# A gated-delta scan on one core: QK loaded and multiplied later, the first units' loads reordered, the last products in halves

## The chip, the cores and the metric

One core of a Trainium2 chip runs the whole program. The metric is the device time in microseconds of one execution; lower is better. The engines are TensorE (PE, with its weight loads PEld), VectorE (DVE), ScalarE (ACT), GpSimd (POOL) and SyncE (SP), which here issues all loads and stores. Each engine works through its own instruction stream in order and waits for others by semaphores.

## What is computed

One layer of a hybrid backbone on 128 context and 2048 latent tokens of width 1024 (17 tiles of 128 tokens): modulated norm, one input projection, a bidirectional chunked gated DeltaNet with 4 heads of 128 beside a gated spatial MLP, an output projection, and a squared-ReLU MLP of width 4096. The change concerns the DeltaNet, whose core in the reference is, for each head, direction and chunk (chunks of 64 in the reference; the kernel works on 128 tokens at a time):

```python
a_mat = where(strict, (k_beta @ k.T) * decay, 0)
sol = triangular_solve(a_mat + eye, [v * beta, k_beta * exp(g)])     # u, w
qk = (q @ k.T) * decay
def step(S, xs):
    v_new = u_c - w_c @ S
    o = qd @ S + qk_c @ v_new
    S = S * exp(gl) + kd.T @ v_new
```

and the last rows of the output, `y + ga2 * (relu(h @ w_ff1)**2 @ w_ff2)` followed by a norm.

## The kernel before

PE multiplies float32 as two rounded halves: `mm3` (L242, L243, L244) issues three matmuls, high x high, the low half of one side (L243) and the low half of the other (L244), into one PSUM bank. Names that end in H and L are such halves (`wH`, `wL`, `hH`, `hL`, `opH`, `opL`); ACT makes the high one by a copy, DVE the low one by a subtraction.

By time, the program has four stages. Up to about 440 us: modulation, norm, and the q, k and v projection with its convolution; KK = k k^T and QK = q k^T of each tile are left in DRAM (`kk_d`, `qk_d`), as are the running sums of the log decays (`g_d`). From about 440 to 1230: the scan, which this text is about. From 1230 to 2592: the two products of the MLP.

The scan has 34 units, 17 tiles forward and then 17 backward; a unit takes some 22 us. Unit i has a preparation, which does not depend on the state, and four chain steps, which do.

- Loads for the preparation (`prep_loads`): `gb`, the sums of the tile's log decays broadcast to all partitions, `KK` and `QK`.
- ACT makes the decays `E` = exp(-|gb - g|) (four Abs by head at L1035, one exp of 128x512 at L1036). POOL cuts it into the strict triangle `Es` (L1038) and the inclusive one, in place in `E` (L1040). DVE multiplies `KK` by beta and `Es` (four products, L1048), POOL sets the diagonal (L1050), ACT rounds to `AH` (L1053), DVE forms `X` (L1054), PE transposes it (L1060) and ACT copies it to `Y` (L1062).
- Five levels s = 2 to 32 of the triangular inverse: PE (L1080), DVE's masked `P` (L1084), PE (L1092, L1094), ACT's copies of `Y` and `X` (L1095, L1096). At s = 2, DVE also multiplies `QK` by `E` (L1098). A sixth level, a correction `R` and the result `T` follow (L1110 to L1139).
- Chain: vt and o from the state (L1151, L1143); `vs` and `vn` (L1164, L1166); the new state `S` (L1178); and QK times vn, added to o (L1192 to L1197). All these quads of matmuls have line L1011.

`KK`, `E` and `Es` share one tag "e" with four buffers, and `QK` has three buffers. Preparation PSUM tiles are `pd`, four banks.

Between these, as filler for PE, run the projections for gate, v and u of the gMLP (`f2`, PSUM tiles `pj` and `pm`, with loaded halves `hH`, `hL` of the normed tile, L1237), and from the backward units on the output projection (`wH,oH`), the norm for the MLP and the first operands of the MLP (`opH`, `opL`, L904 and L905).

The order of all this is set by a list: `at(time, fn)` puts a step at a time in units, the list is sorted, and the code is issued in that order. A scheduler that simulates times then sets each engine's order from it, taking what is ready; a tile's buffers count as ready when their last reader is done. `after_weights(f, names, engines)` adds that f's instructions stand behind those of an earlier group on the named engines. The loads of unit i's preparation stand at i - 3, those of unit 0 at -11.85; `f2[0][0]`, the loads of hH and hL of tile 0, at -9.

At the very end, the last MLP product of the last tile sums four groups q = 0 to 3, of four operands each, into one bank of 512 columns; q = 3 is done in two halves of 256 columns, and after each half `part` (in `final_last`) does the final sums on DVE and ACT.

Of the kernel before, what the change touches and what calls it, by code (L numbers as in the profile page):

```python
# [8 lines left out]
F32 = mybir.dt.float32  # L9
# [4 lines left out]
ALU = mybir.AluOpType  # L14
# [3 lines left out]
P = 128  # L18
# [34 lines left out]
PL = 0  # L53
# [12 lines left out]
def hybrid_step(  # L66
# [143 lines left out]
    done = {}  # L210

    def here():
        return len(tc.nc.cur_bb.bb.instructions)
# [24 lines left out]
    def mm3(ps, trip, first=True, last=True, more=False):  # L238

        n = len(trip)  # L240
        for i, (lh, ll, rh, rl) in enumerate(trip):
            T.matmul(ps, lh, rh, start=first and i == 0, stop=False, skip_group_check=more)  # L242
            T.matmul(ps, lh, rl, start=False, stop=False, skip_group_check=more)  # L243
            T.matmul(ps, ll, rh, start=False, stop=last and i == n - 1, skip_group_check=more)  # L244
# [716 lines left out]
    with ExitStack() as ph:  # L961
# [20 lines left out]
        def q32(tag, bufs=1, pool=None):  # L982
            return (pool or dl).tile([P, 4, P], F32, tag=tag, name=tag, bufs=bufs)

        def s32(name):
            return pp.tile([P, 4, P], F32, tag="e", name=name, bufs=NE)
# [14 lines left out]
        def unit(t, d):  # L1001
# [11 lines left out]
            def prep_loads():  # L1013
                u["gb"] = load_rows(g_d, t, d)
                u["KK"] = s32("KK")
                load(out=u["KK"], in_=kk_d[t])
                u["QK"] = q32("QK", 3)
                load(out=u["QK"], in_=qk_d[t])

            def scan_loads():  # L1020
# [9 lines left out]

            @prep.append
            def _():
                e = s32("E")
                for h in range(H):
                    A.activation(e[:, h, :], u["gb"][:, h, :], AF.Abs, scale=-1.0, bias=col(gcol, h))  # L1035
                A.activation(e, e, AF.Exp, scale=-1.0)  # L1036
                es = s32("Es")
                G.affine_select(out=es, in_=e, pattern=[[0, 4], [-sg, P]], compare_op=ALU.is_gt, fill=0.0,  # L1038
                                base=0, channel_multiplier=sg)
                G.affine_select(out=e, in_=e, pattern=[[0, 4], [sg, P]], compare_op=ALU.is_ge, fill=0.0,  # L1040
                                base=0, channel_multiplier=-sg)
                u["Es"], u["E"] = es, e
# [22 lines left out]
            def level(s):  # L1065

                def half(ap, i):
                    return ap.rearrange("p h (a t b) -> p h a t b", t=2, b=s)[:, :, :, i, :]

                def packed(p, i):  # L1070
                    return p[:, :, i * 64 : i * 64 + 64].rearrange("p h (a b) -> p h a b", b=s)

                yi = 1 - d

                @prep.append
                def _():
                    p = pd()
                    pp, y = packed(p, 0), half(u["Y"], yi)
                    for h in range(H):
                        T.matmul(pp[:, h], u["AH"][:, h, :], y[:, h], start=True, stop=True)  # L1080
                    u["P"] = pms[s]
                    if t == 0:
                        V.tensor_copy(pms[s], identq)
                    V.tensor_tensor(out=half(u["P"], yi), in0=pp, in1=half(bc4(sm[s]), yi), op=ALU.mult)  # L1084

                @prep.append
                def _():
                    p = pd()
                    py, px = packed(p, 0), packed(p, 1)
                    y, x, pm = half(u["Y"], yi), half(u["X"], 1 - yi), half(u["P"], yi)  # L1090
                    for h in range(H):
                        T.matmul(py[:, h], u["X"][:, h, :], pm[:, h], start=True, stop=True)  # L1092
                    for h in range(H):
                        T.matmul(px[:, h], u["P"][:, h, :], x[:, h], start=True, stop=True)  # L1094
                    A.copy(y, py)  # L1095
                    A.copy(x, px)  # L1096
                    if s == 2:
                        V.tensor_tensor(out=u["QK"], in0=u["QK"], in1=u["E"], op=ALU.mult)  # L1098

            for s in (2, 4, 8, 16, 32):  # L1100
                level(s)
# [56 lines left out]
            @scan.append  # L1158
            def _():
                p = pd()  # L1160
                quad(p, u["T"], u["vt"])
                u["vs"] = q32("vs", 1)
                cols = eglg[:, t, d * 4 : d * 4 + 4].unsqueeze(2).to_broadcast([P, 4, P])
                V.tensor_tensor(out=u["vs"], in0=p, in1=cols, op=ALU.mult)  # L1164
                u["vn"] = q32("vn", BT)
                A.copy(u["vn"], p)  # L1166

            @scan.append
            def _():
# [30 lines left out]

            u["t"], u["d"] = t, d
            u["prep"], u["scan"] = prep, scan
            u["prep_loads"], u["scan_loads"] = prep_loads, scan_loads
            return u

        units = [unit(t, 0) for t in range(NT)] + [unit(t, 1) for t in [0] + list(range(NT - 1, 0, -1))]
# [181 lines left out]
        def at(time, fn, kind=None):  # L1388
            events.append((time, len(events), fn, kind))
# [13 lines left out]
        def after(i):  # L1403
# [4 lines left out]
            load(out=s0, in_=state_delta[0, 0, d].rearrange("h k v -> k h v"))  # L1408
            units[i + 1]["s0"] = s0

        def after_weights(f, names, engines):

            start = here()
            f()
            for name in names:
                behind(name, start, engines)

        p2, p3 = WINDOWS[:8], WINDOWS[8:]
        for i, u in enumerate(units):
            w = p2 if i <= NT else p3  # L1420
            at(i - 3 if i > PL else -11.85, u["prep_loads"])
            at(i - 1, lambda i=i, u=u: after_weights(u["scan_loads"], LATER.get(i, ()), (mybir.EngineType.SP,)))
            u["prep"][:2] = [lambda i=i, f=f: after_weights(f, AHEAD_OF.get(i, ()), (mybir.EngineType.Activation,
                                                                                    mybir.EngineType.DVE))
                             for f in u["prep"][:2]]
            n = len(u["prep"])
            for j, st in enumerate(u["prep"]):
                at(i - w[0] + (j + 0.5) * (w[0] - w[1]) / n if i or j > 9 else -11.6 if j < 2
                   else 0.2 * j - 8.15, st, "prep")
            spread(i + w[2], i + w[3], [scan_step(i, f) for f in u["scan"]], "chain")  # L1430
            if i in (0, NT):
                at(i + w[2] + (w[3] - w[2]) * 0.7, lambda i=i: after(i))
            if i >= NT:
                at(i, lambda u=u: o_loads(u))
                first, second = o_steps(u)
                spread(i + p3[4], i + p3[5], first, "fill")
                spread(i + p3[6], i + p3[7], second, "fill")
                if u["t"] > 8:
                    st = h2_steps(u["t"], pj, fraw, w512, fpart, fhalf, lambda u=u: u["x2"])
                    spread(i + p3[8], i + p3[9] + 0.2, st[:5], "fill")  # L1440
                    spread(i + p3[9] + 0.2, i + p3[9] + 2.1, st[5:], None)
# [10 lines left out]
            flat += [(KT * n + j, st) for j, st in enumerate(main)]  # L1452
            flat += [(KT * n + KT + j + (0.5 if n >= HT else -0.5), st) for j, st in enumerate(later)]
        flat = [st for _, st in sorted(flat, key=lambda e: e[0])]
        at(-9, f2[0][0])
        engines = (mybir.EngineType.Activation, mybir.EngineType.DVE)
        for j, st in enumerate(flat[:NF]):
            g, k = divmod(j, KT + 1)
# [53 lines left out]
    def bank():  # L1512
        return psq.tile([P, 512], F32, tag="f", name="f", bufs=8)

    def add(out, a, b, op=ALU.add):
        V.tensor_tensor(out=out, in0=a, in1=b, op=op)  # L1516
# [268 lines left out]
    def final_last(t, y):  # L1785
# [12 lines left out]

        def part(ps, h):
            c = slice(256 * h, 256 * h + 256)  # L1800
            add(x[0][:, c], ps[:, c], ga[0][:, c], ALU.mult)
            add(y[0][:, c], x[0][:, c], y[0][:, c])
            A.activation(x[0][:, c], y[0][:, c], AF.Square, accum_out=ss[:, 2 * h : 2 * h + 1])
            if h == 0:
                V.scalar_tensor_tensor(out=ss[:, 3:4], in0=ss[:, 0:1], scalar=1.0 / D, in1=ss[:, 3:4], op0=ALU.mult,
                                       op1=ALU.add)
# [135 lines left out]
                    s_next(AHEAD + e // 2 - 1, True) if e // 2 < 3 else None  # L1942


    pending = []
    rest = ps = None
    for m, (n, i, u, q) in enumerate(todo):
        us = products[n][1]
# [11 lines left out]
            elif i == 2:  # L1960
                rest = final(0, [y0[0], y0[1]]) if u == 8 else final(pairs[u][0], [acc["x", u], acc["u", u]])
        h, lo = sops.pop(m)
        if m == len(todo) - 1:
            for e in range(2):
                c, e2 = slice(256 * e, 256 * e + 256), slice(2 * e, 2 * e + 2)
                mm3(ps[:, c], [(h[:, kp, :], lo[:, kp, :], t[:, 0, e2], t[:, 1, e2])
                               for kp, t in enumerate(tiles[n][4 * q : 4 * q + 4])], first=False, last=True, more=True)
                rest[0](ps, e)
            rest[1]()
            continue  # L1970
        mm3(ps, [(h[:, kp, :], lo[:, kp, :], t[:, 0, :], t[:, 1, :])
                 for kp, t in enumerate(tiles[n][4 * q : 4 * q + 4])], first=q == 0,
            last=q == (2 if m == len(todo) - 2 else 3))
        if q == 3:
            outcome(i, u, ps)
            if i in (4, 2):
# [65 lines left out]
```

## Time and profile before

| | us |
|---|---|
| median of 3 runs | 2593.64 (2592.26 to 2595.88) |
| the profiled execution, its own time | 2593.88 |
| span of its profile | 2592.0 |
| PE busy | 2549.9 (98%) |
| DVE busy | 1803.9 (70%) |
| ACT busy | 1221.7 (47%) |
| POOL busy | 236.1 (9%) |

The span is the time from the first to the last instruction on the chip; what lies around it is 1.9 us. The granted clock of PE, over the span, is 0.997. PE's line has two parts, matmuls (PE) and the loads of their stationary operand (PEld), which run beside matmuls. A row of the timeline has the start, the duration, the engine, the line, the operation, its tiles and shape, and in brackets how long the engine sat idle before it and what it then waited for. In groups of waits the numbers are the total in us, how many times, and the longest.

### The profile page before, as it was taken

The numbers are of one execution on the slowest core, as the hardware profiler recorded it, in microseconds if no ns is written. First come the engines' busy times: TensorE is split into PE (matmuls) and PEld (weight loads), VectorE is DVE, ScalarE is ACT, GpSimd is POOL, SyncE is SP. The second block draws the span as 40 slices with busy tenths as digits, with TensorE's granted clock in tenths as the row PEclk, the third lists the DMA queues.
The fourth block names the chain that finished last, engine by engine and source line by source line (L and its number), as shares of the span: only waits on it lengthen the run. The fifth ranks groups of instructions, "written<-read, shape, count | busy, mean of one in ns | idle before, by whom it ended". The sixth has DMA issues, their size and how long they took to land.

```text
span 2592.0 us, 44687 instructions
## 1 busy us (share of the span) xinstructions
PE 2549.9 (98%) x15520; PEld 2156.4 (83%) x15520; DVE 1803.9 (70%) x3738; ACT 1221.7 (47%) x3051; POOL 236.1 (9%) x448
## 2 busy tenths in 40 slices
PE   9999999999999999999999999999999999999998
PEld 5899999788888787788888888888888888888887
DVE  5867756676677878886678876666675557784875
ACT  4755555555555667764345543333342432342442
POOL 3112212111111111210000000000000000000000
PEclk9999999999999999999999999999999999999999
DMA  8977737654455657885768789444479979786683
GB/s 283 303 219 210 212 111 250 219 161 145 151 155 163 206 173 241 277 278 183 278 204 260 225 282 304 115 117 118 122 234 368 340 264 333 261 257 205 225 268 106
DMA packets 494695, 571.88 MB, mean 221 GB/s; under 512 B 35124, under 2 KB 297564, under 8 KB 490886
## 3 DMA queue, kind: packets, MB, share of 16 engines
q1 hardware_dynamic: 494470, 569.04, 67.5%
q8 instruction: 122, 2.00, 0.3%
q14 instruction: 103, 0.84, 0.1%
HBM read 389.23 MB, written 179.67 MB: 219 GB/s over the span
## 4 chain that ended last, share of the span: by engine, by line
PE 88%; DMA 4%; DVE 4%; ACT 2%; issue 1%; SPq 1%; POOL 0%; POOLq 0%; ACTq 0%; DVEq 0%
PE f L242 16%; PE f L244 16%; PE f L243 16%; PE pj L242 7%; PE pj L244 7%; PE pj L243 7%; PE pd L1011 5%; PE f L1636 2%; PE pm L242 1%; PE pm L244 1%; PE pm L243 1%; PE pt L626 1%; DMA raw<-in_w_mod_dram 1%; PE pt L585 1%; PE pd L1092 1%
## 5 line engine op out<-in xcount | busy, mean ns | idle before, releaser
L242 PE MATMUL f<-hop,zH 128*128 128x512 f32 (+1 forms) x964 | 374.2, 388 | 1.7 <-ACT zH L1522 1.2
L243 PE MATMUL f<-hop,zH 128*128 128x512 f32 (+1 forms) x964 | 374.0, 388 | 0.0
L244 PE MATMUL f<-hop,zL 128*128 128x512 f32 (+1 forms) x964 | 373.9, 388 | 0.0
L242 PE MATMUL f<-hop,wH 128*128 128x512 f32 x896 | 355.4, 397 | 0.1
L243 PE MATMUL f<-hop,wH 128*128 128x512 f32 x896 | 349.1, 390 | 0.0
L244 PE MATMUL f<-hop,wL 128*128 128x512 f32 x896 | 347.9, 390 | 0.0
L1522 ACT CAST zH<-zraw 128x512 fp32r<-128x512 f32 x240 | 146.6, 620 | 283.7 <-DVE zraw L1516 85.7
L242 PEld LDWEIGHTS f<-hop,zH 128*128 128x128 f32 x964 | 180.9, 188 | 39.6 <-ACT zH L1522 1.6
L244 PEld LDWEIGHTS f<-hop,zL 128*128 128x128 f32 x964 | 180.9, 188 | 37.7 <-DVE zL L1516 0.4
L243 PEld LDWEIGHTS f<-hop,zH 128*128 128x128 f32 x964 | 181.0, 188 | 37.5 <-issue 0.2
L1516 DVE TENSOR_TENSOR zL<-zraw,zH 128x512 fp32r<-128x512 f32 x240 | 162.8, 687 | 67.3 <-ACT zH L1522 54.2
L244 PEld LDWEIGHTS f<-hop,wL 128*128 128x128 f32 x896 | 168.2, 188 | 35.3
L242 PEld LDWEIGHTS f<-hop,wH 128*128 128x128 f32 x896 | 168.5, 188 | 32.7 <-issue 0.5
L243 PEld LDWEIGHTS f<-hop,wH 128*128 128x128 f32 x896 | 168.5, 188 | 32.4
L242 PE MATMUL pj<-kH,wH 128*128 128x386 f32 (+2 forms) x568 | 190.5, 338 | 1.8 <-ACT junk L602 1.1
L244 PE MATMUL pj<-kH,wL 128*128 128x386 f32 (+2 forms) x568 | 189.7, 335 | 0.0
L243 PE MATMUL pj<-kL,wH 128*128 128x386 f32 (+2 forms) x568 | 189.4, 335 | 0.0
L185 POOL TENSOR_TENSOR r<-rsq,nhalf 128x1 f32<-128x1 f32 (+1 forms) x37 | 25.1, 678 | 1417.0 <-DVE rsq L184 1417.0
L572 DVE SCALAR_TENSOR_TENSOR cv<-pj,vec,cv 128x384 f32<-128x384 f32 (+2 forms) x164 | 87.0, 539 | 51.7 <-ACT cv L569 50.4
L242 PEld LDWEIGHTS pj<-kH,wH 128*128 128x128 f32 x568 | 107.1, 189 | 5.2 <-issue 2.4
L1522 ACT CAST wH<-s 128x512 fp32r<-128x512 f32 x96 | 59.4, 621 | 105.4 <-DVE s L1516 103.2
L243 PEld LDWEIGHTS pj<-kL,wH 128*128 128x128 f32 x568 | 107.4, 189 | 0.6
(410 smaller groups left out, 5712.1 us busy)
## 6 DMA issues: line engine op xcount, KB each, us to landing
zraw<-z_d SPq DMA_DIRECT2D x212, 256.0 KB
raw<-in_w_ff_dram SPq DMA_DIRECT2D x128, 256.0 KB
hop<-hop_d SPq DMA_DIRECT2D x28, 1024.0 KB
z_d<-c SPq DMA_DIRECT2D x96, 256.0 KB
zraw<-s_d SPq DMA_DIRECT2D x96, 256.0 KB
raw<-in_w_mod_dram SPq DMA_DIRECT2D x80, 256.0 KB
r<-in_w_ff_dram SPq DMA_DIRECT2D x80, 256.0 KB
s_d<-s SPq DMA_DIRECT2D x64, 256.0 KB
```

The source lines that it names most:

```text
L185: G.tensor_tensor(out=out, in0=t[:np_, :n], in1=nhalf[:np_, :n], op=ALU.pow)
L242: T.matmul(ps, lh, rh, start=first and i == 0, stop=False, skip_group_check=more)
L243: T.matmul(ps, lh, rl, start=False, stop=False, skip_group_check=more)
L244: T.matmul(ps, ll, rh, start=False, stop=last and i == n - 1, skip_group_check=more)
L572: V.scalar_tensor_tensor(out=cv[:, o : o + m], in0=ps[:, s + sh : s + sh + m], scalar=convw[:, w, j : j + 1], in1=cv[:, o : o + m], op0=AL ...
L585: T.transpose(pq[:, i * P : (i + 1) * P], u["x2"][:, i * P : (i + 1) * P], ident)
L626: T.matmul(ps[:, i * P : (i + 1) * P], kTt[:, i * P : (i + 1) * P], rhs[:, i * P : (i + 1) * P], start=True, stop=True)
L1011: T.matmul(p[:, h, :], lhs[:, h, :], rhs[:, h, :], start=True, stop=True)
L1092: T.matmul(py[:, h], u["X"][:, h, :], pm[:, h], start=True, stop=True)
L1516: V.tensor_tensor(out=out, in0=a, in1=b, op=op)
L1522: A.copy(h, src)
L1636: T.matmul(ps[:, c : c + P], self.raw[m, kh][:, kp, :], x0[kh][:, kp, :], start=first and kp == 0, stop=last and kp == 3)
```

## The change

QK's load leaves `prep_loads`. It is a step of its own, `qk_load`, one unit ahead of the chain and not three, into two buffers and not three. Its multiply by E leaves level s = 2 and stands in the second chain step, behind the copy of vn. E gets a tag of its own with three buffers, so the four of "e" hold KK and Es. For units 0 and 1 both preparations' sums and KK are loaded at -12.1, QK of both behind KK of unit 1, and the loads of hH and hL of tile 0 behind KK of unit 1 too. At the end the whole last product (four groups) is done in two halves of 256 columns, each in a bank of its own.

```diff
@@ prep_loads
                 load(out=u["KK"], in_=kk_d[t])
-                u["QK"] = q32("QK", 3)
+
+            def qk_load():
+                u["QK"] = q32("QK", 2)
                 load(out=u["QK"], in_=qk_d[t])
@@ decays
-                e = s32("E")
+                e = pp.tile([P, 4, P], F32, tag="E", name="E", bufs=3)
@@ level
-                    if s == 2:
-                        V.tensor_tensor(out=u["QK"], in0=u["QK"], in1=u["E"], op=ALU.mult)
@@ second chain step
                 A.copy(u["vn"], p)
+                V.tensor_tensor(out=u["QK"], in0=u["QK"], in1=u["E"], op=ALU.mult)
@@ events
+        def noted(name, f):
+
+            start = here()
+            f()
+            done[name] = tc.nc.cur_bb.bb.instructions[start:]
...
-            at(i - 3 if i > PL else -11.85, u["prep_loads"])
+            at(i - 3 if i > 1 else -12.1, lambda i=i, u=u: noted(("kk", i), u["prep_loads"]))
+            at(i - 1 if i > 1 else -11.1, lambda i=i, u=u: after_weights(
+                u["qk_load"], (("kk", 1),) if i < 2 else (), (mybir.EngineType.SP,)))
...
-        at(-9, f2[0][0])
+        at(-9, lambda: after_weights(f2[0][0], (("kk", 1),), (mybir.EngineType.SP,)))
@@ final_last, part
-            add(x[0][:, c], ps[:, c], ga[0][:, c], ALU.mult)
+            add(x[0][:, c], ps[:, 0:256], ga[0][:, c], ALU.mult)
@@ last products
-        if m == len(todo) - 1:
-            for e in range(2):
-                c, e2 = slice(256 * e, 256 * e + 256), slice(2 * e, 2 * e + 2)
-                mm3(ps[:, c], [(h[:, kp, :], lo[:, kp, :], t[:, 0, e2], t[:, 1, e2])
-                               for kp, t in enumerate(tiles[n][4 * q : 4 * q + 4])], first=False, last=True, more=True)
-                rest[0](ps, e)
-            rest[1]()
+        if m >= len(todo) - 4:
+
+            def columns(ps, e, q, h, lo):
+                c = slice(2 * e, 2 * e + 2)
+                mm3(ps[:, 0:256], [(h[:, kp, :], lo[:, kp, :], t[:, 0, c], t[:, 1, c])
+                                   for kp, t in enumerate(tiles[n][4 * q : 4 * q + 4])], first=q == 0, last=q == 3)
+
+            columns(ps, 0, q, h, lo)
+            ends.append((q, h, lo))
+            if q == 3:
+                rest[0](ps, 0)
+                ps = bank()
+                for e in ends:
+                    columns(ps, 1, *e)
+                rest[0](ps, 1)
+                rest[1]()
             continue
```

How the order on the engines changes is best seen at two places. The first is SP's queue at the start of the scan; `raw` are filler weights, `vt_d` and `gate_d` stores of results, `hH` and `hL` the tiles for the v projection. Before, four rows stand ahead of these: gb of unit 0 (row 357), a store vt_d, QK of unit 0 and a raw. Then:

```order
361 L590 DMA vt_d<-tk 128x2x128 x2
362 L191 DMA raw<-in_w_in_dram 128x512
363 L1237 DMA hH<-hH_d 128x512 x2
364 L1237 DMA hL<-hL_d 128x512
365 L1016 DMA KK<-kk_d 128x512
366 L1237 DMA hL<-hL_d 128x512
367 L1254 DMA gate_d<-th 128x512
368 L1237 DMA hH<-hH_d 128x512 x2
369 L191 DMA raw<-in_w_in_dram 128x512
370 L1237 DMA hL<-hL_d 128x512 x2
371 L191 DMA raw<-in_w_in_dram 128x512
372 L991 DMA gb<-g_d 128x512
```

After, behind gb of unit 0 (row 357) and a store vt_d:

```order
359 L991 DMA gb<-g_d 128x512
360 L191 DMA raw<-in_w_in_dram 128x512
361 L590 DMA vt_d<-tk 128x2x128 x2
362 L191 DMA raw<-in_w_in_dram 128x512
363 L1016 DMA KK<-kk_d 128x512 x2
364 L1255 DMA gate_d<-th 128x512
365 L1020 DMA QK<-qk_d 128x512 x2
366 L191 DMA raw<-in_w_in_dram 128x512
367 L1238 DMA hH<-hH_d 128x512 x2
368 L191 DMA raw<-in_w_in_dram 128x512
369 L1238 DMA hL<-hL_d 128x512 x2
```

The second gb, that of unit 1, moves from row 372 to row 359, KK and QK of both units stand at rows 363 and 365, and hH and hL of tile 0 go from rows 363 to 366 to rows 367 to 369. With a row's x2 counted as two, and gb of unit 0 as the first, gb of unit 1 goes from place 20 to 3, KK of unit 0 from 11 to 8, and the first hL from 10 to 17.

The second place is DVE's order around a pair of level masks P of two units in the backward part (near 1008 us of the trace). Lines of after are one to two higher than those of before: L1048 is L1050, L1084 is L1086, L1333 is L1334. Before:

```order
1257 L184 TENSOR_SCALAR rsq<-r_14058 128x4
1258 L1048 SCALAR_TENSOR_TENSOR KK<-KK,beta,Es 128x128
1259 L905 TENSOR_TENSOR opL<-y,opH 128x512
1260 L1048 SCALAR_TENSOR_TENSOR KK<-KK,beta,Es 128x128 x3
1261 L1084 TENSOR_TENSOR P_5794<-pd,sm_186 128x8x32
1262 L1084 TENSOR_TENSOR P_5791<-pd,sm_183 128x64x4
1263 L1330 TENSOR_TENSOR r_15556<-rq 128x4
1264 L1164 TENSOR_TENSOR vs<-pd,eglg 128x512
1265 L905 TENSOR_TENSOR opL<-y,opH 128x512
1266 L1333 SCALAR_TENSOR_TENSOR rr<-rr,rq 128x4
```

And after:

```order
1260 L1331 TENSOR_TENSOR r_15550<-rq 128x4
1261 L905 TENSOR_TENSOR opL<-y,opH 128x512
1262 L1334 SCALAR_TENSOR_TENSOR rr<-rr,rq 128x4
1263 L1086 TENSOR_TENSOR P_5794<-pd,sm_186 128x8x32
1264 L1086 TENSOR_TENSOR P_5791<-pd,sm_183 128x64x4
1265 L1164 TENSOR_TENSOR vs<-pd,eglg 128x512
1266 L1336 SCALAR_TENSOR_TENSOR o<-o,rr,ga 128x128 x4
1267 L905 TENSOR_TENSOR opL<-y,opH 128x512
1268 L1050 SCALAR_TENSOR_TENSOR KK<-KK,beta,Es 128x128 x4
```

KK's four products, ahead of the two masks before, stand five rows behind them after; rr, which waits for POOL, now stands ahead of them. Over the whole program QK's load and multiply move to about one unit (22 us) later, and the multiply still stands some 40 us ahead of the product that uses it; PE's own order is the same up to about 900 us but for small swaps, and from there on the filler groups move by some 3 us. The set of instructions is the same on every engine but PE, which has 36 more matmuls.

More of the change, by code (lines that the diff above doesn't have):

```diff
@@ L1202, in unit @@
             u["prep"], u["scan"] = prep, scan
-            u["prep_loads"], u["scan_loads"] = prep_loads, scan_loads
+            u["prep_loads"], u["scan_loads"], u["qk_load"] = prep_loads, scan_loads, qk_load
             return u
@@ L1942, in hybrid_step @@
                     s_next(AHEAD + e // 2 - 1, True) if e // 2 < 3 else None
-    pending = []
+    pending, ends = [], []
     rest = ps = None
@@ L1962, in hybrid_step @@
         h, lo = sops.pop(m)
-        if m == len(todo) - 1:
-            for e in range(2):
-                c, e2 = slice(256 * e, 256 * e + 256), slice(2 * e, 2 * e + 2)
-                mm3(ps[:, c], [(h[:, kp, :], lo[:, kp, :], t[:, 0, e2], t[:, 1, e2])
-                               for kp, t in enumerate(tiles[n][4 * q : 4 * q + 4])], first=False, last=True, more=True)
-                rest[0](ps, e)
-            rest[1]()
+        if m >= len(todo) - 4:
[12 more added lines that the diff above has]
+                rest[1]()
             continue
         mm3(ps, [(h[:, kp, :], lo[:, kp, :], t[:, 0, :], t[:, 1, :])
-                 for kp, t in enumerate(tiles[n][4 * q : 4 * q + 4])], first=q == 0,
-            last=q == (2 if m == len(todo) - 2 else 3))
+                 for kp, t in enumerate(tiles[n][4 * q : 4 * q + 4])], first=q == 0, last=q == 3)
         if q == 3:
```

## The prediction

> **What bounds it now.** I read the page first: busy shares and the chain that ended last.
>
> ```profile
> PE 2549.9 (98%) x15520; PEld 2156.4 (83%) x15520; DVE 1803.9 (70%) x3738; ACT 1221.7 (47%) x3051; POOL 236.1 (9%) x448
> PE 88%; DMA 4%; DVE 4%; ACT 2%; issue 1%; SPq 1%; POOL 0%; POOLq 0%; ACTq 0%; DVEq 0%
> ```
>
> TensorE bounds the kernel, so an edit can gain what PE idles, or lose by a new idle. Next the busy time by stretches: the scan stage (440 to 1230) holds PE's gaps. A row has the stretch, its length, the busy time of PE, weight loads, DVE, ACT and POOL (with counts), the granted clock, the DMA share and GB/s.
>
> ```profile
> 440.00:500.00 60.00, 55.57 (x374) 43.74 (x373) 41.91 (x120) 32.62 (x79) 13.67 (x17) 0.94 0.76 264
> 1000.00:1230.00 230.00, 218.51 (x1886) 181.63 (x1886) 183.60 (x448) 145.88 (x456) 35.99 (x37) 1.00 0.72 245
> ```
>
> Third, what PE waited for: in this order 440 to 500, 500 to 893, 893 to 904, 904 to 1000 and 1000 to 1235 (us in total, times, longest).
>
> ```profile
> PE pd L1080 <- ACT Y L1062: 4.1, 1, 4.1
> ...
> PE pd L1092 <- DVE P L1084: 3.5, 4, 1.2
> ...
> PE pd L1080 <- ACT Y L1095: 1.8, 2, 1.6
> ...
> PE pm L1348 <- DVE o L1335: 0.3, 1, 0.3
> PE pj L1348 <- DVE o L1335: 0.3, 1, 0.3
> ...
> PE pd L1092 <- DVE P L1084: 4.9, 5, 1.4
> PE pd L1080 <- ACT Y L1095: 4.5, 7, 1.3
> ```
>
> So what can be won in the scan is some 15 to 20 us: waits for the level masks P (DVE) and for Y (ACT), and one wait of 4.1 us at unit 0.
>
> **The start (unit 0 and 1).**
>
> ```profile
> 449.13 1.14 DVE L1048 SCALAR_TENSOR_TENSOR KK<-KK,beta,Es 128x128 f32<-128x128 f32 x4 [4.28 <-DMA KK<-kk_d]
> 451.54 0.39 PE L244 MATMUL pm<-wH,hL 128*128 128x512 f32 x1
> 452.54 0.40 PE L1060 MATMUL pd<-ident,X 128*128 128x128 f16 x4
> 453.58 0.62 ACT L202 CAST wH<-raw 128x512 fp32r<-128x512 f32 x1 [0.54 <-DMA raw<-in_w_in_dram]
> 453.98 0.40 PE L244 MATMUL pm<-wH,hL 128*128 128x512 f32 x1
> 456.22 1.28 ACT L1035 ACTIVATE E<-gb,gcol 128x128 f32<-128x128 f32 x4 [2.01 <-DMA gb<-g_d]
> 457.91 0.57 ACT L1062 CAST Y<-pd 128x512 f16<-128x512 f32 x1
> 458.53 0.37 PE L1080 MATMUL pd<-Y,AH 128*128 128x64 f16 x4 [4.15 <-ACT Y L1062]
> ```
>
> pd of L1060 was written by 453, but ACT, in order, stood at unit 1's decays (L1035) until their sums gb landed at 456.2, and Y of unit 0 came behind. After, gb of unit 1 is third in SP's queue from gb of unit 0 on, where it was twentieth, so this wait goes. But what stood ahead of it in the queue goes back. Counted from gb of unit 0 as 1, KK of unit 0 moves from 11 to 8, the first hL of the v projection from 10 to 17. The order has room for it only if landings follow the queue: 11 landed by 449.1, 16 (raw) by 453.54, 20 (gb) by 456.2; from 16 to 20 that is 0.66 us for each place. Then hL, at 17, lands at 454.2, and PE, in order, waits at L244 from 451.54 to 454.2: 2.7 us, new. L1060 and the projections behind it shift by 2.7 us and end by 457.0; Y of unit 0 takes 0.57 us on a free ACT behind L1060 (455.2) and is there by 456.2. So L1080 starts at 457.0 and not at 458.53: 1.5 us gained. KK, X and AL of both units stay hidden in that wait; if they come later than hL, L1060 waits instead, so the lower end is no gain. If hL lands in time, the whole 4.15 us go.
>
> The clock hangs on it:
>
> ```profile
> 453.08:456.49 3.41, 1.30 (x6) 0.82 (x5) 1.84 (x3) 0.90 (x2) 0.00 (x0) 1.00 1.05 400
> 456.49:459.90 3.41, 1.37 (x7) 1.18 (x7) 1.27 (x3) 2.95 (x8) 0.75 (x2) 0.50 1.07 380
> 459.90:463.32 3.42, 3.42 (x17) 2.42 (x16) 2.65 (x6) 1.08 (x4) 2.15 (x2) 0.50 1.00 354
> 507.69:511.10 3.41, 2.27 (x18) 2.25 (x19) 1.71 (x7) 0.21 (x1) 0.00 (x0) 1.00 0.20 58
> ```
>
> With PE busy for 1.30 us of a stretch, the granted clock was 0.50 from 456.49 to 463.3; with 2.27 busy it stayed 1.00. PE worked from 458.7 to 463.3 at half clock, 4.6 us for what full clock does in 2.3. A wait of 2.7 us that falls into one such stretch leaves 0.7 busy and halves the clock; split over two it doesn't. About an even chance, so half of 2.3: the start gains 1.5 + 1.2 = **2.7** (ends: 0, and 4.15 + 2.3 = 6.4). The Trainium skill, "TensorE: Matmul & The Clock Gate", Part 1, says that the clock falls after at least one idle window of some 3.4 us, windows running free. This trace halved it with 1.30 us of work in the window, so I don't go by that reading; by it a wait of 2.7 us would never halve the clock, and the start would gain 3.8.
>
> **QK loaded and multiplied later.** Work on DVE and the load count stay the same, 34 each.
>
> ```profile
> 623.04 1.05 PE L1011 MATMUL pd<-vn,QK 128*128 128x128 f32 x8
> 624.12 0.32 SPq L1018 DMA_DIRECT2D QK<-qk_d  x1
> 626.97 0.69 DVE L1098 TENSOR_TENSOR QK<-QK,E 128x512 f32<-128x512 f32 x1 [1.03 <-DMA QK<-qk_d]
> DVE QK L1098 <- DMA QK<-qk_d: 24.1, 22, 2.4
> POOL Es L1038 <- DVE QK L1098: 191.7, 17, 19.4
> ```
>
> The load was issued as soon as the product of three units earlier had left a buffer, and DVE multiplied 2.9 us later. With two buffers the order puts both a unit (22 us) later, again just behind the release and the multiply some 4 us behind the load; DVE's 24.1 us of waits stay, costed at no change (ends: gone, or doubled). What changes is behind it: E's buffers were held until the multiply, and POOL's Es, then KK on DVE, came in whenever it ended. Now E has three of its own, and KK moves behind the masks that PE waits for. DVE at 1006 to 1010, which carries the longest of these waits:
>
> ```profile
> 1006.49 0.81 DVE L1048 SCALAR_TENSOR_TENSOR KK<-KK,beta,Es 128x128 f32<-128x128 f32 x1
> 1007.12 1.05 POOL L185 TENSOR_TENSOR rr<-rsq,nhalf 128x4 f32<-128x4 f32 x1
> 1007.83 0.86 DVE L1048 SCALAR_TENSOR_TENSOR KK<-KK,beta,Es 128x128 f32<-128x128 f32 x3
> 1008.61 0.74 DVE L1084 TENSOR_TENSOR P<-pd,sm 128x256 f16<-128x256 f32 x2
> 1009.08 0.29 PE L1092 MATMUL pd<-P,X 128*128 128x64 f16 x4 [1.37 <-DVE P L1084]
> 1004.51 0.28 PE L1080 MATMUL pd<-Y,AH 128*128 128x64 f16 x4 [1.25 <-ACT Y L1095]
> 895.43 0.28 PE L1080 MATMUL pd<-Y,AH 128*128 128x64 f16 x4 [1.55 <-ACT Y L1095]
> ```
>
> KK's 0.81 + 0.86 = 1.67 us stand ahead of P before, and behind it after; against that DVE now takes rr ahead of P, which waits for POOL's 1.05 us. So of the 1.37 us here about half goes. At 610, 808, 828, 877, 1055, 1101 and 1147 it is KK or QK that leaves the place ahead of P, with nothing else put there: 3.5 us in 500 to 893, nine tenths counted: **3.2**. 1000 to 1235: for P 4.9 less the 0.7 just named, 4.2. Of Y's 4.5, E's exp on ACT goes behind Y, but at 1004 opH also stood ahead of it and stays there, so half: 2.2. Together **6.4**. In 904 to 1000 **0.6** (two transposes that waited 0.3 for o). Lost: near 895 exp of unit 22 now stands ahead of Y (a pass of that size takes ACT 0.57 us, as L1062 above), +0.6, and four products of o ahead of P, of which a wait for POOL hid about half (KK's four took 1.67, so some 0.8 less what is already idle), +0.6: **1.2**. The three gains are 10.2; their lower end is a fifth (2), where the next late releaser takes over, the upper the whole of those rows (13.5).
>
> Every wait that goes leaves the next one bare, and KK, later on DVE by a microsecond or two, gives AH, X and Y later. Nothing of before shows the size; bounds are zero and the 10.2 just counted. Of the eight places of P one (1006) has something else put ahead, and half of it was given back; an eighth of 10.2 is 1.3, and with the waits that KK's delay may bring I take **2.0**.
>
> **The tail.** Four products of the last tile, in halves of 256 columns, half 0 whole and then half 1 in a bank of its own.
>
> ```profile
> 2580.44 0.39 PE L244 MATMUL f<-hop,zL 128*128 128x512 f32 x1
> 2580.67 0.39 PE L242 MATMUL f<-hop,zH 128*128 128x512 f32 x1
> 2582.54 0.28 PE L243 MATMUL f<-hop,zH 128*128 128x256 f32 x1
> 2582.66 0.28 PE L244 MATMUL f<-hop,zL 128*128 128x256 f32 x1
> 2583.46 0.39 PE L242 MATMUL f<-hop,zH 128*128 128x256 f32 x1 [0.52 <-DVE x L1516]
> ```
>
> 36 matmuls of 512 (0.227 each) become 72 of 256 (0.12 each): 36 x 0.013 = 0.47 more. The stall at 2583.46, where half 1 waited until DVE had read half 0 from the same bank, goes: 0.80 from the matmul ahead, less the usual 0.12, is 0.68. Net **0.2** gained (ends: 0.5 lost if the stall stays, 0.4 gained). DVE's work on half 0 lies beside half 1, which is now 48 matmuls long; what follows PE's end is as before.
>
> Sum: -2.7 - 3.2 - 6.4 - 0.6 + 1.2 + 2.0 - 0.2 = -9.9. The profiled execution took 2593.88 us (span 2592.0), the median of the runs is 2593.64, so the sum holds for both: 2593.9 - 9.9 = **2584.0**.
>
> **Rivals.**
> (a) The places are taken over: PE's new wait for hL with a halved clock eats the start (0), and in the scan the next releaser keeps all but 3 us of the waits: -3 + 1.2 + 2.0 - 0.2 = 0, so 2591 to 2596. For it: ACT and DVE take turns between Y and P, and in 1000 to 1230 DVE is busy for 183.60 of 230 us, ACT for 145.88. Against: at seven places KK or QK leaves P's front with no substitute.
> (b) Slower: QK's load waits on SP, in order, for the product two units back, and what is behind it on SP (kt, kT, qT of later units) waits too; DVE's multiply now stands in the scan step, ahead of masks of a later unit. If the load lands late, DVE stands still, then P and PE. DVE's longest such wait was 2.4 us; 2 us more in each of 34 units are 68, and if a third of it reaches PE, 22 us: 2584 + 22 = 2606. It decides where PE loses more than 9.9 / 34 = 0.3 us for a unit. For it: the load at 624.12 stands right behind the product that frees its buffer. Against: the multiply isn't late itself. The product of the unit loaded at 624 comes three units, some 66 us, behind that at 623, and the multiply a unit later than at 627 still stands some 40 us ahead.
> (c) Nearly all goes: hL in time and the clock whole (6.4), 12 of the scan's 13.5, and no half clock behind 895 (some 3 us): 2593.9 - 6.4 - 12 - 3 + 1.2 - 0.2 = 2573, up to 2577.
> That the change doesn't do what its words say (the multiply still stands some 40 us ahead of its use, not just ahead) is so in the order, and is costed as it stands there.
>
> **Chances.** The forecast (2577 to 2589) 0.63, (a) 0.18, (b) 0.09, (c) 0.10. A change of 0.2%, 5.2 us, is what a measurement of this kernel can tell. Faster: 0.63 + 0.10, 0.73; same: nearly all of (a), 0.17; slower: (b) and the rest, 0.10. The range leaves out most of (b) and the ends of (c): 2575 to 2593.5; the likeliest case alone is 2577 to 2589.
>
> **What would show it.** Right: waits of PE for P (9.0 us in all) under 4, for Y under 5; E's L1035 of unit 1 no longer waiting 2.01 us at 456; a wait of PE at L244 near 451.5 for hL; POOL's 191.7 us for QK gone; no DVE wait at the tail's L242. Wrong: a new group of over 5 us among PE's waits in the scan; DVE's waits for QK above 45 us; PE's clock at half in more stretches than now.

## The result and the profile after

The changed kernel takes 2596.84 us (median of 20 runs, 2590.96 to 2603.35), the kernel before 2592.35 us in the 20 runs taken with it (2587.35 to 2595.88). The ratio is 1.0019 with a 95% interval of 1.0012 to 1.0026: some 5 us slower, where 9.9 us of gain were forecast. Beside the experiments below it was timed again: 2596.39 against 2590.82, 1.0021 (1.0012 to 1.0030).

The page after, busy shares and the chain:

```profile
PE 2546.0 (98%) x15556; PEld 2156.4 (83%) x15556; DVE 1798.9 (69%) x3738; ACT 1221.0 (47%) x3051; POOL 234.8 (9%) x448
PE 85%; DMA 5%; DVE 5%; ACT 2%; issue 1%; POOL 1%; SPq 0%; POOLq 0%; DVEq 0%; ACTq 0%
```

PE's share of the chain fell from 88% to 85%: more of the end is now set by others. By stretches (same columns as before):

```profile
440.00:500.00 60.00, 56.44 (x416) 43.89 (x416) 44.85 (x124) 33.81 (x85) 16.02 (x18) 1.00 0.76 266
1000.00:1230.00 230.00, 215.37 (x1840) 180.49 (x1838) 173.34 (x430) 140.57 (x438) 32.50 (x36) 0.99 0.71 238
```

At the start PE is busier (56.44 us, 55.57 before) and the clock stays whole; in the backward half it idles more (215.37 busy, 218.51 before). What PE waited for, in 440 to 500, 500 to 893, 893 to 1000 and 1000 to 1235 (lines of after are two higher here: L1082 is L1080, L1094 is L1092, L1097 is L1095):

```profile
PE pm L244 <- DMA hL<-hL_d: 1.2, 1, 1.2
PE pd L1094 <- DVE P L1086: 1.1, 1, 1.1
PE pd L1082 <- ACT Y L1064: 1.0, 1, 1.0
...
PE pd L1094 <- DVE P L1086: 3.1, 6, 0.6
PE pd L1082 <- ACT Y L1097: 2.7, 3, 2.1
PE pd L1110 <- ACT Y L1097: 1.9, 1, 1.9
...
PE pd L1082 <- ACT Y L1097: 2.7, 5, 0.9
...
PE pd L1082 <- ACT Y L1097: 8.9, 11, 2.1
PE pj L244 <- DVE oL L1353: 4.1, 3, 1.4
PE pd L1094 <- DVE P L1086: 0.6, 2, 0.3
```

In the last stretch the waits for P went from 4.9 to 0.6 us, as forecast; in 500 to 893 they hardly fell, from 3.5 to 3.1. The waits for Y in the last stretch doubled, from 4.5 to 8.9, and 4.1 us for oL are new. All of PE's waits in 440 to 1235 add up to some 25.5 us before and 31.8 after. The reason for Y's stands in ACT's own waits. Before, after, and POOL after (440 to 1235):

```profile
ACT E L1035 <- DVE AL L1063: 8.4, 12, 1.2
```

```profile
ACT E L1037 <- DVE QK L1167: 28.5, 22, 4.1
POOL Es L1040 <- ACT E L1038: 238.2, 27, 18.8
```

Before, it was POOL that waited for QK's multiply (191.7 us, 17 times), an engine with 9% of work. After, POOL waits for ACT, and ACT waits for the multiply. Before, at the same unit, E had no wait, and Y was there in time:

```profile
1020.57 1.28 ACT L1035 ACTIVATE E<-gb,gcol 128x128 f32<-128x128 f32 x4
1022.07 1.14 ACT L1143 ACTIVATE o<-pd,neg 128x128 f32<-128x128 f32 x4
1023.71 1.14 ACT L1139 ACTIVATE T<-pd,hbeta 128x128 f32<-128x128 f32 x4
1024.72 0.39 ACT L1095 CAST Y<-pd 128x256 f16<-128x256 f32 x1
```

The timeline of after from 1010 to 1022 shows what the new wait does:

```profile
1010.73 0.61 PE L1011 MATMUL pd<-vn,QK 128*128 128x128 f32 x4
1011.55 0.44 SPq L1020 DMA_DIRECT2D QK<-qk_d  x1
1017.32 0.69 DVE L1167 TENSOR_TENSOR QK<-QK,E 128x512 f32<-128x512 f32 x1 [1.90 <-DMA QK<-qk_d]
1018.05 1.28 ACT L1037 ACTIVATE E<-gb,gcol 128x128 f32<-128x128 f32 x4 [3.94 <-DVE QK L1167]
1019.24 1.11 ACT L1143 ACTIVATE o<-pd,neg 128x128 f32<-128x128 f32 x4
1020.24 1.14 ACT L1139 ACTIVATE T<-pd,hbeta 128x128 f32<-128x128 f32 x4
1021.24 0.41 ACT L1097 CAST Y<-pd 128x256 f16<-128x256 f32 x1
1021.69 0.28 PE L1082 MATMUL pd<-Y,AH 128*128 128x64 f16 x4 [1.94 <-ACT Y L1097]
```

Read it downwards. The product of two units back leaves a QK buffer; SP issues the load; DVE waits 1.90 us for it and multiplies at 1017.32; only then is a buffer of E free, for the unit three later; ACT, which had come to that E in its order, has stood still for 3.94 us; o, T and Y stand behind it; and PE waits for Y. The same comes back two units later, at 1067.7, and two more on, at 1115.9: these three make 12 of ACT's 28.5 us.

Such a wait can take the clock along:

```profile
1019.87:1023.28 3.41, 1.32 (x17) 1.22 (x16) 3.41 (x11) 3.41 (x12) 0.22 (x1) 1.00 0.67 193
1023.28:1026.69 3.41, 3.41 (x12) 2.71 (x12) 2.05 (x7) 0.91 (x3) 1.69 (x3) 0.51 0.43 145
```

PE was busy for 1.32 of 3.41 us, and the next 3.41 us ran at half clock. The waits at 1067.7 and 1115.9 took nothing of the clock. The profiled execution (2592.45 us, span 2590.7, mean clock 0.999) has only this one stretch of half clock in the scan, where the profile of before has two of 6.8 us each (from 456.5 and 896.8), and is among the fastest four of the 20. Seven runs with a mean clock of 0.997 average 2598.5 us, ten with 0.998 average 2594.6: its profile shows the waits, but less of the lost clock than most runs have. That is one reason why its span is not longer than that of before. The other lies in the untouched first 440 us, in which PE was busy for 435.5 us in this execution and for 432.6 in that of before.

### The profile page after: what moved, and what is told of

Its sections match the earlier page's. It is cut to its first block, busy times and chain, and to the rows that moved or that the text cites. A ratio compares the mean times of both kernels' runs of the same rounds, so it can differ in the third digit from the quotient of the medians.

```text
span 2590.7 us, 44726 instructions
## 1 busy us (share of the span) xinstructions
PE 2546.0 (98%) x15556; PEld 2156.4 (83%) x15556; DVE 1798.9 (69%) x3738; ACT 1221.0 (47%) x3051; POOL 234.8 (9%) x448
## 4 chain that ended last, share of the span: by engine, by line
PE 85%; DMA 5%; DVE 5%; ACT 2%; issue 1%; POOL 1%; SPq 0%; POOLq 0%; DVEq 0%; ACTq 0%
PE f L242 16%; PE f L244 16%; PE f L243 16%; PE pj L242 7%; PE pj L244 6%; PE pj L243 6%; PE pd L1011 4%; PE f L1645 2%; PE pm L242 1%; DMA QK<-qk_d 1%; PE pm L244 1%; PE pm L243 1%; PE pt L626 1%; DMA hop_d<-opL 1%; DMA raw<-in_w_mod_dram 1%
```

## The experiments

All are timed against the kernel before on the same chip (2590.71 us for the first four, 2590.82 for the next four, 2592.02 for the last two). Between kernels of different sets the ratios are the safer comparison. A ratio and the two medians beside it can differ by 0.06%, or 1.5 us. Three of the kernels (four buffers for E, E in its own tag, and early multiply with E behind Y) need room, and so also leave out the constant `identq`, which their few copies into the masks now read by broadcast.

**The scan part alone.** Loads of units 0 and 1 and the last products as before:

```diff
 # the changed kernel, with
-            at(i - 3 if i > 1 else -12.1, lambda i=i, u=u: noted(("kk", i), u["prep_loads"]))
+            at(i - 3 if i > PL else -11.85, u["prep_loads"])
...
-        at(-9, lambda: after_weights(f2[0][0], (("kk", 1),), (mybir.EngineType.SP,)))
+        at(-9, f2[0][0])
```

> The kernel before with the scan part of the change alone (QK loaded one unit ahead into two buffers and multiplied behind vn, E with a tag of three buffers); the loads of units 0 and 1 and the last products stay as before. Theory: the scan part is what loses. E of unit n+3 needs the buffer that the multiply of unit n frees, the multiply waits for QK's load, the load for the product two units back; ACT waits in order with o, T and Y behind it. Expected: ACT's waits for the multiply 25 to 30 us, PE's waits for Y 13 to 16 us (6.5 before), P's 4 to 6 (9.0 before), time 2 to 8 us above before. Rival A: the scan part is even, and the new wait for hL at the start with a halved clock loses: then within 2 us of before.

Measured: 2598.36 us, ratio 1.0027 (1.0017 to 1.0037), 7.7 us slower. ACT waited 29.7 us for the multiply, PE 15.9 for Y and 3.8 for P. All are near what was expected: the scan part is what loses.

**The start alone.** The kernel before with the new loads of units 0 and 1:

```diff
 # the kernel before, with qk_load as its own step (three buffers), and
-            at(i - 3 if i > PL else -11.85, u["prep_loads"])
+            at(i - 3 if i > 1 else -12.1, lambda i=i, u=u: noted(("kk", i), u["prep_loads"]))
+            at(i - 3 if i > 1 else -11.1, lambda i=i, u=u: after_weights(
+                u["qk_load"], (("kk", 1),) if i < 2 else (), (mybir.EngineType.SP,)))
...
-        at(-9, f2[0][0])
+        at(-9, lambda: after_weights(f2[0][0], (("kk", 1),), (mybir.EngineType.SP,)))
```

> The kernel before with the loads at the start alone (sums and KK of units 0 and 1 first, their QK behind, hL of tile 0 behind KK); QK of the other units loaded and multiplied as before. Theory: gains 2 to 4 us against before (the wait of 4.1 us at unit 0 becomes one of 1 to 3 us for hL), 2588 to 2590. Rival A: a wait for hL halves the clock in most runs and eats it or more: 0 to 4 us above before.

Measured: 2586.05 us, 0.9982 (0.9973 to 0.9990), 4.7 us faster, a little more than expected. PE waited 0.9 us for hL, and in the profile the clock stayed whole through the scan.

**Four buffers for E.** The changed kernel with

```diff
-                e = pp.tile([P, 4, P], F32, tag="E", name="E", bufs=3)
+                e = pp.tile([P, 4, P], F32, tag="E", name="E", bufs=4)
```

> The changed kernel with four buffers for E in place of three (the room comes from a constant, an identity of 128x512 in half precision that is now read by broadcast). The order on the engines is nearly the same, only the buffer's release is one unit earlier. Theory: ACT's waits for the multiply fall from 28.5 us to under 8, PE's waits for Y from 14.4 to 5 to 9, and the time falls 4 to 9 us below the changed kernel, to 2588 to 2592. Rival B: the waits for Y come from the new order of steps on ACT and not from E's buffer: Y stays above 12 us and the time is that of the changed kernel, 2595 to 2598.

Measured: 2591.69 us, 1.0005 (0.9997 to 1.0014), by the ratios some 4 us below the changed kernel. The time lies in the expected range, but by luck, since the reason given did not hold:

```profile
PE pd L1080 <- ACT Y L1095: 14.0, 19, 2.5
```

```profile
ACT E L1035 <- DVE QK L1165: 26.9, 23, 4.4
```

ACT waits as long as before, only for a multiply of four units back and not three: with one buffer more the scheduler puts E a unit earlier, just where its simulated time has the buffer free. Here the number of buffers set which multiply is waited for, not whether. PE's waits in the scan add up to 27.3 us, 4.5 fewer than in the changed kernel; why is not settled, and the missing `identq` is not ruled out.

**E in its own tag, QK early.** Start and tail of the change, E in its own tag, but the load at i - 3 and the multiply at level 2, as before:

```diff
 # start and tail, and
-                e = s32("E")
+                e = pp.tile([P, 4, P], F32, tag="E", name="E", bufs=3)
```

> The kernel before with the start and the last products of the change, and with E in a tag of its own with three buffers, but QK loaded three units ahead into three buffers and multiplied at level 2 as before (the same constant left out for room). Theory: the multiply frees E early, ACT does not wait for it (under 8 us), KK stands behind P as in the change, so P's and Y's waits together fall below 9 us (15.5 before): 2584 to 2588. Rival B: the order that goes with E's own tag loses by itself: Y's waits above 12 us, 2592 to 2598.

Measured: 2591.60 us, 1.0003 (0.9995 to 1.0012). By the waits this is the second of the two outcomes, with a time just below its range: the tag loses by itself. ACT waits 25.9 us for the multiply, although it comes a unit earlier, since E comes a unit earlier too:

```profile
PE pd L1080 <- ACT Y L1095: 13.3, 15, 3.2
```

```profile
ACT E L1035 <- DVE QK L1098: 25.9, 20, 5.2
```

So my theory that the late multiply makes E wait was wrong in this part; what makes it wait is that E's buffer hangs on the multiply at all and that E stands ahead of Y on ACT.

**Start and tail.** The kernel before with both, the scan as it was (the diff is that of the start and of the last products).

> The kernel before with the start and the last products of the change, the scan as before. Theory: start and tail gain, the scan part loses: 4 to 6 us below before, and some 6 us below the kernel with E in its own tag as well. Rival: the parts depend on each other (phase of the clock, landing times), and with the tail the gain of the start is not seen: within 2 us of before.

Measured: 2586.80 us, 0.9987 (0.9978 to 0.9996). Against the start alone (0.9982) the tail can't be seen. E's own tag on top of this costs 4.8 us by the medians (2591.60) and 4.1 by the ratios, whose intervals just touch. PE's waits in the scan point the same way: 29.3 us with the tag, 22.1 without.

**E behind Y on ACT.** The changed kernel, with one order added; no buffer and no wait is taken away:

```diff
             n = len(u["prep"])
+            u["prep"][4] = lambda i=i, f=u["prep"][4]: noted(("y2", i), f)
+            if i > 2:
+                u["prep"][0] = lambda i=i, f=u["prep"][0]: after_weights(f, (("y2", i - 2),),
+                                                                         (mybir.EngineType.Activation,))
```

> The changed kernel, with one added order on ACT: the decays E of unit i stand behind the copies of Y and X at level 2 of unit i - 2 (no wait is taken away, only the place in ACT's stream changes). Theory: ACT no longer stands at the multiply with Y behind it: ACT's waits of E for the multiply fall from 28.5 to under 8 us, PE's waits for Y from 14.4 to 4 to 8, and the time falls 4 to 8 us below the changed kernel. Rival: E, later, makes KK and X late, and PE waits elsewhere (L1062 or the level behind it): time as the changed kernel or above.

Measured: 2578.41 us, 0.9958 (0.9946 to 0.9971): 18 us below the changed kernel in the same set (2596.39), and 11 to 12 below before. Expected were 4 to 8 us below the changed kernel: the waits came out as expected, and the time fell more than twice as far. PE's waits in the scan add up to 18.2 us against 31.8, which is 13.6 of the 18; the rest is not accounted for. PE's waits, ACT's wait, and the same place as in the timeline above:

```profile
PE pd L1082 <- ACT Y L1097: 4.6, 8, 1.6
PE pj L244 <- DVE oL L1353: 4.1, 3, 1.4
PE pd L1094 <- DVE P L1086: 2.1, 6, 0.6
```

```profile
ACT E L1037 <- DVE QK L1167: 1.5, 2, 0.8
```

```profile
1008.17 0.69 DVE L1167 TENSOR_TENSOR QK<-QK,E 128x512 f32<-128x512 f32 x1 [1.75 <-DMA QK<-qk_d]
1009.28 0.41 ACT L1097 CAST Y<-pd 128x256 f16<-128x256 f32 x1
1009.80 0.45 ACT L1097 CAST Y<-pd 128x256 f16<-128x256 f32 x1
1010.33 1.36 ACT L1037 ACTIVATE E<-gb,gcol 128x128 f32<-128x128 f32 x4
```

DVE still waits 1.75 us for QK; ACT does o, T and Y meanwhile, and finds the buffer free when it comes to E. Y's waits went from 14.4 to 4.6, P's from 5.5 to 2.1. Half clock is not what it saved: this profile has two such stretches in the scan, the changed kernel's one.

**KK behind P on DVE.** Start and tail on the kernel before, E in the shared tag, and the order that the forecast had counted on:

```diff
+            u["prep"][5] = lambda i=i, f=u["prep"][5]: noted(("p4", i), f)
+            if i > 2:
+                u["prep"][1] = lambda i=i, f=u["prep"][1]: after_weights(f, (("p4", i - 2),),
+                                                                         (mybir.EngineType.DVE,))
```

> Start and tail of the change on the kernel before, and one added order on DVE: the four products KK of unit i stand behind the mask P at level 4 of unit i - 2. E, Es and KK share their four buffers as before, QK is loaded and multiplied as before. It does by itself what the forecast counted on from E's tag. Theory: PE's waits for P fall from 9 us to under 4, Y's stay near 6, time 3 to 6 us below the kernel with start and tail alone. Rival: the waits move to Y or to KK's followers, and the sum of PE's waits in the scan stays within 2 us.

Measured: 2583.54 us, 0.9973 (0.9964 to 0.9982), 3.3 us below start and tail. Both outcomes in part: P's waits fell from 10.0 to 3.0, and the wait of the sixth level (L1112) for its Y grew from 1.1 to 4.7:

```profile
PE pd L1082 <- ACT Y L1097: 5.2, 10, 1.6
PE pd L1112 <- ACT Y L1097: 4.7, 7, 1.4
PE pd L1094 <- DVE P L1086: 3.0, 7, 0.9
```

**The changed kernel again**, beside the three above.

> The changed kernel once more, beside the others on one chip: 3 to 7 us above before; its profile again with ACT's waits for the multiply near 28 us and Y's waits of PE of 13 to 16 us, and one to three stretches of half clock in the scan.

Measured: 2596.39 us. ACT waited 30.0 us for the multiply, PE 14.4 for Y, 5.8 for P and 4.1 for oL; one stretch of half clock in the scan, at 897.6.

**Early multiply, E behind Y.** The order of ACT as in the kernel with E behind Y, on E's own tag with QK loaded and multiplied early.

> Start and tail of the change, E in its own tag with three buffers, E of unit i behind Y of level 2 of unit i - 2 on ACT, but QK loaded three units ahead and multiplied at level 2 as before. PE's order is that of the kernel with the late multiply and E behind Y, so the pair shows what the late load and multiply are worth by themselves. Theory: nothing (within 3 us of it, 2576 to 2582), since the multiply stands 40 us ahead of its use either way; and E's own tag alone, which lost 5 us against start and tail, gains with E behind Y. Rival: the late multiply is what gains, and this kernel is 4 us or more above it.

Measured: 2578.77 us, 0.9947 (0.9933 to 0.9961), the same as with the late multiply (0.9958) within the noise, which is some 5 us for this pair. With E behind Y the tag that had cost 4 to 5 us gains 8 to 10 against start and tail. Against E in its own tag, from which it differs by this order alone, the kernel gains 13 to 15. No worth of the time of QK's load and multiply can be seen by itself.

**hL ahead of KK.** The kernel with E behind Y, and

```diff
-        at(-9, lambda: after_weights(f2[0][0], (("kk", 1),), (mybir.EngineType.SP,)))
+        at(-9, f2[0][0])
```

> The changed kernel with E behind Y and with one order less on SP: hH and hL of tile 0 are not put behind KK of unit 1, and go ahead of it. Theory of the start: PE's wait for hL (1.2 us) goes, KK of the units lands some 2 us later and is still in time or gives back less than that: 0 to 2 us below the kernel with E behind Y, 2576 to 2579. Rival: unit 0 waits for KK instead, by more than hL cost: 1 to 4 us above it.

Measured: 2583.63 us, 0.9967 (0.9955 to 0.9980), 5 us slower by the medians than with hL behind KK (2578.41). By the ratios it is 2 us, and the intervals overlap, so the time alone does not settle it; the waits are those of the second outcome. hL no longer waits; unit 0 does, for X (after KK) and then for Y:

```profile
PE pd L1062 <- DVE X L1056: 2.0, 1, 2.0
PE pd L1082 <- ACT Y L1064: 1.9, 1, 1.9
```

## Why the prediction was wrong

- **The start** was right in kind and too small: 2.7 forecast, 4.7 measured alone (2.6 to 7.0 by its interval). The wait of 4.15 us for Y of unit 0 became one of 1.0, and PE waits for hL as forecast, but for 1.2 us and not 2.7, and the clock stays whole. In two profiles with the same loads, four buffers for E and E in its own tag, PE waited 1.8 us for hL, and the clock did fall for one stretch there. (The landing of raw put at 453.54 stands at 453.58 in its row; the estimate is the same.)

```profile
450.75 0.50 PE L244 MATMUL pm<-wH,hL 128*128 128x512 f32 x1 [1.23 <-DMA hL<-hL_d]
454.63 0.28 PE L1082 MATMUL pd<-Y,AH 128*128 128x64 f16 x4 [1.00 <-ACT Y L1064]
```

- **P** was right in the last stretch alone, where 4.2 were counted and the waits went from 4.9 to 0.6. In 500 to 893, 3.2 were counted and 0.4 came: near the old places waits of 0.33 and 0.55 are left, but new ones of 0.4 to 0.6 stand at 520, 628, 671 and 718; at the first three of these KK's four products stand one or two steps ahead of P on DVE. So KK left P's front at some places and came to it at others. In all the waits fell by 3.5 us (9.0 to 5.5) where 7.4 were counted. That even 7 us less waiting for P is worth some 3 us is what the kernel with KK behind P shows.
- **Y is the step that failed.** I wrote that E's exp on ACT goes behind Y and counted half of Y's 4.5 us as gained. From 970 on it did so in every other unit, with E's four Abs (L1037) ahead of it, and there PE's waits for Y (1004, 1052, 1097 and 1143 of before) fell by 1.7 us of the 2.2 counted. In the units between, E's Abs stayed in front of o, T and Y, as they had stood before without a wait (1020.57 above). Now they wait there for QK's multiply, and PE has 6.9 us of waits for Y that were not there (around 1021.7, 1071.3 and 1119.5). That E's Abs could wait had no term in the sum. I had read the release of E's buffer only from POOL's side, where 191.7 us of waiting went. In the shared tag E took the buffer of the previous unit's KK, free once AL is made (8.4 us of waits), and Es took that of the E of two units back, so POOL waited for that unit's multiply. With a tag of its own, E takes the buffer of the E of three units back, and ACT waits for the multiply. The wait did not go; it moved from POOL to an engine with Y behind it. Rival (a), that the next releaser keeps what P gives back, is nearest in time and partly right in the scan, but not at the start, which gained. Rival (b) has the chain of load, multiply and buffer, but puts the wait on DVE, whose waits for QK did not change (24.1 before, 24.5 after).
- **New waits**: 2.0 were counted, for KK's delay. Y rose by 8 us over the scan, and oL brought 4.1, which no step had: near 1006 DVE does three products of S ahead of oL. With E behind Y that wait is still 4.1, so it does not come from ACT's wait. Every kernel with E in its own tag has it (3.0 to 4.1), and none with the shared tag, so it goes with the order that the tag brings. In 904 to 1000 the two waits for o went, as counted (0.6), but 2.5 us for Y came.
- **Around 895** 1.2 us were to be lost. PE's waits there rose from 2.4 us (893 to 904, before) to 3.8 (888 to 897, after), 1.4 more. What it costs in time no run tells apart, since a stretch of half clock there comes and goes between runs of one kernel (897.6 in one profile of the changed kernel, none in the other).
- **The tail**: its stall is gone. Half 0's sums start while PE is in half 1, and no wait stands between them; 0.2 us is below what the runs can tell.

```profile
2577.88 0.28 PE L244 MATMUL f<-hop,zL 128*128 128x256 f32 x1
2578.00 0.28 PE L242 MATMUL f<-hop,zH 128*128 128x256 f32 x1
2578.20 0.42 DVE L1525 TENSOR_TENSOR x<-f,row 128x256 f32<-128x256 f32 x1 [0.33 <-PE f L244]
```

- **QK later** was costed at nothing, and nothing can be seen of it (2578.77 and 2578.41 with E behind Y). What matters here is not when QK is multiplied but who has to wait for it.

Of the signs of a right forecast, those at the start and the tail came true, and POOL's wait for the multiply went; P (5.5) and Y (14.4) missed theirs. Of the signs of a wrong one, Y's waits went over 5 us, though as a group that grew and not as a new one. DVE's waits for QK and the count of half-clock stretches in the profile did not go that way. What is open: why a fourth buffer for E gains some 4 us with the same wait on ACT, why E behind Y gains more than the waits it takes away, and how much of the changed kernel's 5 us is lost clock. PE's waits alone rose by 6.3 us in its profile.

## What to carry to other kernels

When a tile moves to another set of buffers, write down for each engine that allocates from it whose last read it will now wait for, and what stands behind that engine's instruction in its order. A long wait on an idle engine can be what keeps a busy one free; taking it away moves the wait, and it is paid where something urgent is queued. When a scheduler works by simulated times, one buffer more may only move the allocation up to the next release, as it did here; an order that puts the waiting instruction behind the urgent one was worth more (18 us here for one added order).

## What was not expected of the hardware

The granted clock halves after stretches of PE work of quite different size, and not always. After 1.32 us busy of 3.41 in the changed kernel it fell for one stretch, and in the kernel before, after 1.30, for two. With E behind Y it fell after 2.10 us busy (1105.47 to 1108.88), and in the second profile of the changed kernel it stayed whole after 1.52 (1020.45 to 1023.86). So the prediction's reading, half clock after 1.30 us and full clock after 2.27, gives no threshold. At that place PE waited 2.74 us for Y, more than the 1.94 us that halved the clock in the first profile, but the wait lay across two stretches (1.52 and 2.29 us busy). The stretches do not start at the same place of the program in each run: counted from the first instruction, they are shifted by some 0.5 us between these two profiles. So the same wait can cost a different time. The runs of the changed kernel spread over 12.4 us (20 runs), those of the kernel with E behind Y over 3.3 (five).
